# Block-distance products for the inner weights of gated linear attention, and paired weight halves in two small projections

## The chip, the cores and the metric

The kernel runs on one core of a Trainium2 chip. The metric is device microseconds from launch to end; three runs gave 1918.55, 1923.94 and 1927.39 us, median 1923.94 us.

## The reference

One layer of a hybrid decoder: 1024 prompt tokens and 64 sample tokens (8 sequences of 8), 1088 in all, model width 1024. After adaLN and an RMSNorm one input projection feeds two head groups: gated linear attention (GLA, 4 heads, keys of 64, values of 128) and a sparse attention of 8 heads with compressed blocks, selected blocks and a window. One output projection joins them; a squared-ReLU MLP follows. What the change touches:

```
logf = log_sigmoid(za @ gla_w_gate + gla_b_gate) / 16          # za: 16 columns of the input projection
chunks of 16 tokens:  b = cumsum(logf);  q_in = q*exp(b);  k_in = k*exp(-b);  k_out = k*exp(b_last - b)
a_intra = causal(q_in @ k_in^T)                                # within a chunk of 16
s = s*exp(b_last) + k_out^T v                                  # state carried from chunk to chunk
hid = silu(z_first + z_second + b1);  kc, vc = hid @ w2 + b2   # compressed keys and values
gates = sigmoid(zg)                                            # 24 gate columns of the input projection
```

## The kernel before

TensorE has no fast product of two f32 operands of full precision, so most products are split: `split` (L250) writes a high part in fp32r (ScalarE, L251) and the remainder in fp32r (VectorE, L252), and `mm3` (L254) issues three matmuls, high x high, low x high, high x low (L257, L258, L259; which operand is the weight varies). Plain f32 matmuls are used for small things; in the trace a plain f32 matmul is two records, a transpose one.

The eight PSUM banks go by tag (`bank`, L232): two `mm`, two `dn`, three `g`, one `av`. A tile asked for under a tag waits until an older one of that tag is free. The order of the instructions on every engine is set by a planner that simulates the program in time; the two GLA functions stand under a high priority, so that their instructions are taken as soon as they can run, and the projections fill what TensorE has left.

- `first_phase` (L342) compresses the samples' cached pages: for each of 8 sequences, one key half and one value half. The value half ends with `hid @ w2` (L519): for each of 2 heads and 2 halves f of the hidden width an `mm3` with the hidden tile as weight and 64 columns of `w2` moving, twelve matmuls of 64 columns, then one VectorE addition of the bias into `vc` and two DMAs on POOL's queue. Loads of the adaLN weight (`w_ada`, 512 KB each) run beside it. `cw2h` and `cw2l` hold the high and low part of `w2`; the value part is stored twice side by side. `compressed_keys` (L1017) has the same twelve matmuls once for the prompt.
- `project_gla` (L731) projects token chunks of 384, 384 and 320 columns. The unit `w_za` has 56 weight columns (16 for `za`, 16 unused, 24 gates): 24 matmuls per chunk by `mm3`. ScalarE copies 16 rows into `za` (whose 17th row is ones, for the bias) and takes the tanh of 24 rows; transposes (L743) turn the gates into token rows in a `dn` bank, which VectorE turns into `gates` (L753). The first chunk is projected while the other two are still being normed.
- `gla` (L828) works through the 1024 tokens in 8 tiles of 128. `log_decay` (L813) forms the decay for two tiles by f32 matmuls of 17 rows (L820). From cumulative sums it makes `eb`, `enb`, `eo` (`k_out`), the block sums `E`, and `QB`, the scaled queries with each head's rows alone. The 128x128 weights of a tile, for 4 heads, go block by block: for each pair p of heads, one VectorE product makes `KI`, 128 keys as each of the 8 query blocks sees them (128x1024, L883); POOL overwrites the 8 own blocks with `enb` (L886); 8 f32 matmuls have one [128x128] slice of `KI` as weight and 32 columns of `QB` moving (2 heads x 16 queries, L888). Four predicated copies (L893) put the causal part into `A`, which is zero elsewhere. Then follow output (L898, L900), norm, transposes (L915) and the state (L919, L924, L931).
- Around these tiles TensorE does the rest of `project_gla` and `project_kv`, in `mm` banks.

The lines of the inner weights:

```
for j in range(8):
    nc.gpsimd.tensor_copy(KI[:, j, j], enb[:, p, 16 * j:16 * j + 16])
for j in range(8):
    nc.tensor.matmul(pa[:, p, j], KI[:, j].rearrange("p a b -> p (a b)"), QB[:, p, j], start=True, stop=True)
```

Of the kernel before, what the change touches and what calls it, by code (L numbers as in the profile page):

```python
# [9 lines left out]
F32 = mybir.dt.float32  # L10
F32R = mybir.dt.float32r
# [30 lines left out]
def shape_constants():  # L42
# [22 lines left out]
    c["causal"] = (j <= i).astype(np.float32)  # L65
# [8 lines left out]
    c["ones"] = np.ones((128, 128), np.float32)  # L74
    return c, big
# [144 lines left out]
class Prog:  # L220
# [121 lines left out]
    def first_phase(self):  # L342
        nc, tc, a = self.nc, self.tc, self.a
        with ExitStack() as st:
# [42 lines left out]
            def tables():  # L387
# [5 lines left out]
                self.split(self.cw2h, self.cw2l, w2)  # L393
                pos = self.small[:, 162:194].rearrange("p (k t) -> p k t", k=2)
# [53 lines left out]
            def compress(b, kind, first):  # L448
# [64 lines left out]
                else:  # L513

                    ps = self.bank("g")
                    x = [y.rearrange("p f (h n) -> p f h n", h=2) for y in (hh, hl)]
                    for h in range(2):
                        for f in range(2):
                            self.mm3(ps[:, h * 64:(h + 1) * 64], [y[:, f, h] for y in x],  # L519
                                     (self.cw2h[:, 1, f, :64], self.cw2l[:, 1, f, :64]), f == 0, f == 1)  # L520
                    vc = t([128, 128], "vc", bufs=1)
                    nc.vector.tensor_tensor(vc, ps[:, :128], self.small[:, 34:162], op=OP.add)
# [3 lines left out]
            for i, (b, kind) in enumerate([(b, kind) for b in range(6) for kind in range(2)] + [(6, 0), (7, 0), (6, 1), (7, 1)]):  # L526
# [12 lines left out]
                if 2 <= i < 14:  # L539
                    ada_chunk(i - 2)  # L540

# [83 lines left out]
    def main_phase(self):  # L625
        nc, tc, a = self.nc, self.tc, self.a
        ffn = ExitStack()
        with ExitStack() as top:
# [3 lines left out]
            with ExitStack() as left, ExitStack() as mid:  # L632
# [5 lines left out]
                self.za = self.t(gp, [17, NT], F32, "za")  # L638
# [92 lines left out]
    def project_gla(self, pool, xs):  # L731
# [3 lines left out]
        for cis in (slice(0, 1), slice(1, 3)):  # L735
            F = lambda i: zip(self.feat_linear(a["w_f"][i], 128, xs[cis]), CHUNKS[cis])
            for ps, (c0, npr, n) in zip(self.feat_linear(a["w_za"], 56, xs[cis]), CHUNKS[cis]):
                nc.scalar.copy(self.za[:16, c0:c0 + n], ps[:16])
                gt = self.t(pool, [128, 384], F32, "st", 2)[:24, :n]
                nc.scalar.activation(gt, ps[32:56], AF.Tanh, scale=0.5)  # L740
                for o in range(0, n, 128):
                    w = min(128, n - o)
                    nc.tensor.transpose(pg[:w, (c0 + o) // 128], gt[:, o:o + w], self.C("ident")[:24, :24])  # L743
# [8 lines left out]
        for d, x in ((self.gates, pg[:, :8]), (self.gates_s, pg[:NS, 8])):  # L752
            nc.vector.tensor_scalar(d, x, 0.5, 0.5, op0=OP.mult, op1=OP.add)  # L753
# [74 lines left out]
    def gla(self, st):  # L828
# [3 lines left out]
        self.wg = t([17, 256], "wg")  # L832
        nc.sync.dma_start(self.wg, self.a["wg"])
        QBs, As, qis = ([t(sh, f"{x}{i}") for i in range(k)]
                        for sh, x, k in (([128, 2, 8, 2, 16], "QB", 2), ([128, 4, 128], "A", 2),
                                         ([128, 2, 2, 8, 16], "qi", 1)))
# [881 lines left out]
```

## Time and profile before

| | |
|---|---|
| median of three runs | 1923.94 us (1918.55 to 1927.39) |
| profiled execution | 1928.44 us, span 1926.8 us |
| TensorE matmul records | 1834.3 us busy, 12185 |
| VectorE / ScalarE / GpSimd busy | 1131.1 / 935.2 / 361.6 us |
| mean granted TensorE clock | 0.965 of full speed |
| DMA | 246 MB, mean 128 GB/s |

Times are microseconds from the start of the span. Engines: PE is the matmuls of TensorE, PEld its weight loads, DVE VectorE, ACT ScalarE, POOL GpSimd. Matmuls overlap: the duration printed for one holds its way through the array, so the time from one start to the next is what one costs in a row of them. PEclk is the granted clock as a share of full speed; a stretch at 0.50 runs at 1.2 GHz, one at 1.00 at 2.4 GHz.

### The profile page before, as it was taken

The numbers are of one execution on the slowest core, as the hardware profiler recorded it, in microseconds if no ns is written. First come the engines' busy times: TensorE is split into PE (matmuls) and PEld (weight loads), VectorE is DVE, ScalarE is ACT, GpSimd is POOL, SyncE is SP. The second block draws the span as 40 slices with busy tenths as digits, with TensorE's granted clock in tenths as the row PEclk, the third lists the DMA queues.
The fourth block names the chain that finished last, engine by engine and source line by source line (L and its number), as shares of the span: only waits on it lengthen the run. The fifth ranks groups of instructions, "written<-read, shape, count | busy, mean of one in ns | idle before, by whom it ended". The sixth has DMA issues, their size and how long they took to land.

```text
span 1926.8 us, 33628 instructions
## 1 busy us (share of the span) xinstructions
PE 1834.3 (95%) x12185; PEld 1645.7 (85%) x12185; DVE 1131.1 (59%) x2499; ACT 935.2 (49%) x1889; POOL 361.6 (19%) x622
## 2 busy tenths in 40 slices
PE   4999999999999999999999899999999999999997
PEld 4888889999989756456687699899999999999996
DVE  7866775355433574345545746956566668755555
ACT  4423354243333477366655656534433464654443
POOL 4433202124410355245222200000000001000000
PEclk8999999989999899699999899999999999999998
DMA  7667641103464504233112356412121245664442
GB/s 252 217 233 237 210 137 45 34 31 102 142 211 154 187 12 140 68 111 110 50 59 66 105 191 195 145 55 77 44 88 56 76 155 159 206 203 153 149 148 93
DMA packets 117149, 246.01 MB, mean 128 GB/s; under 512 B 14443, under 2 KB 72589, under 8 KB 116182
## 3 DMA queue, kind: packets, MB, share of 16 engines
q1 hardware_dynamic: 101206, 196.98, 32.4%
q0 software_dynamic: 13328, 43.99, 6.6%
q10 hardware_dynamic: 2448, 2.88, 0.4%
q8 instruction: 96, 1.57, 0.3%
q14 instruction: 71, 0.58, 0.1%
HBM read 215.88 MB, written 32.05 MB: 129 GB/s over the span
## 4 chain that ended last, share of the span: by engine, by line
PE 80%; DMA 6%; DVE 6%; ACT 3%; issue 3%; SPq 1%; POOL 1%; POOLq 0%; ACTq 0%; DVEq 0%
PE mm L257 11%; PE mm L259 11%; PE mm L258 11%; PE dn L257 5%; PE dn L258 5%; PE dn L259 5%; PE av L1154 4%; PE g L1149 4%; PE g L258 3%; PE g L257 3%; PE g L259 3%; PE dn L1126 2%; DMA wr<-w_ada 2%; PE dn L1127 2%; PE mm L1296 1%
## 5 line engine op out<-in xcount | busy, mean ns | idle before, releaser
L252 DVE TENSOR_TENSOR wl<-wr,wh 128x1024 fp32r<-128x1024 f32 (+1 forms) x176 | 215.0, 1222 | 202.0 <-ACT wh L251 200.6
L251 ACT CAST wh<-wr 128x1024 fp32r<-128x1024 f32 (+1 forms) x176 | 183.3, 1042 | 239.4 <-PE mm L258 111.2
L257 PE MATMUL dn<-fh,wh 128*128 128x384 f32 (+1 forms) x616 | 206.3, 336 | 2.6 <-DVE fo L1559 1.7
L258 PE MATMUL dn<-fl,wh 128*128 128x384 f32 (+1 forms) x616 | 205.5, 334 | 0.0
L259 PE MATMUL dn<-fh,wl 128*128 128x384 f32 (+1 forms) x616 | 205.2, 334 | 0.0
L586 POOL TENSOR_TENSOR rs_r<-rs_m,mhalf 128x2 f32<-128x2 f32 (+2 forms) x12 | 12.9, 1078 | 709.6 <-DVE rs_m L585 709.5
L257 PE MATMUL mm<-hT,wh 128*128 128x384 f32 (+3 forms) x408 | 138.2, 339 | 5.3 <-DVE st L765 3.3
L258 PE MATMUL mm<-hT,wh 128*128 128x384 f32 (+3 forms) x408 | 136.8, 335 | 0.0
L259 PE MATMUL mm<-hT,wl 128*128 128x384 f32 (+3 forms) x408 | 136.7, 336 | 0.0
L257 PEld LDWEIGHTS dn<-fh,wh 128*128 128x128 f32 x616 | 115.7, 188 | 4.7 <-DVE fo L1559 2.7
L258 PEld LDWEIGHTS dn<-fl,wh 128*128 128x128 f32 x616 | 115.7, 188 | 0.3 <-DVE fl L252 0.3
L259 PEld LDWEIGHTS dn<-fh,wl 128*128 128x128 f32 x616 | 115.7, 188 | 0.1
L1151 ACT COPY pw<-g 128x512 f32<-128x512 f32 (+3 forms) x148 | 81.7, 585 | 59.9 <-PE g L1149 58.7
L1559 DVE TENSOR_TENSOR fo<-fo,dn 128x384 f32<-128x384 f32 (+1 forms) x134 | 72.4, 541 | 59.6 <-PE dn L259 58.9
L257 PE MATMUL mm<-w1h,wh 128*128 128x256 f32 x256 | 77.4, 302 | 19.8 <-ACT wh L251 14.9
L1154 PE MATMUL av<-pw,VV 128*64 128x256 f32 x528 | 86.8, 413 | 1.9 <-ACT pw L1151 1.8
L257 PEld LDWEIGHTS mm<-hT,wh 128*128 128x128 f32 (+1 forms) x408 | 77.0, 189 | 8.3 <-DVE st L765 4.4
L1126 PE MATMUL dn<-KK,QS 128*128 128x512 f32 (+3 forms) x192 | 77.7, 409 | 6.5 <-DVE mx L1129 6.3
L257 PE MATMUL mm<-cth,wh 128*128 128x256 f32 (+1 forms) x256 | 76.0, 298 | 5.2 <-ACT cth L251 4.7
L257 PE MATMUL mm<-x2h,wh 128*128 128x320 f32 x256 | 79.2, 309 | 0.0
L259 PE MATMUL mm<-x2h,wl 128*128 128x320 f32 x256 | 79.2, 309 | 0.0
L258 PE MATMUL mm<-x2l,wh 128*128 128x320 f32 x256 | 79.1, 309 | 0.0
(597 smaller groups left out, 5461.0 us busy)
## 6 DMA issues: line engine op xcount, KB each, us to landing
wr<-w_up SPq DMA_DIRECT2D x72, 512.0 KB, 3.6
wr<-w_down SPq DMA_DIRECT2D x72, 512.0 KB, 3.6
wr<-w_ada SPq DMA_DIRECT2D x48, 512.0 KB, 4.4
wr<-w_f SPq DMA_DIRECT2D x24, 512.0 KB, 3.8
wr<-cw SPq DMA_DIRECT2D x16, 512.0 KB, 4.4
wr<-w_out SPq DMA_DIRECT2D x16, 512.0 KB, 3.6
raw<-cc SPq DMA_DIRECT2D x62, 128.0 KB, 3.8
raw<-cc POOLq DMA_DIRECT2D x61, 128.0 KB, 4.9
```

The source lines that it names most:

```text
L251: return (self.nc.scalar.copy(h, src), (lo or self.nc.vector).tensor_tensor(l, src, h.bitcast(F32), op=OP.subtract))
L252: (lo or self.nc.vector).tensor_tensor(l, src, h.bitcast(F32), op=OP.subtract))
L257: mm(out, ah, bh, start=start, stop=False)
L258: mm(out, ah, bl, start=False, stop=False)
L259: mm(out, al, bh, start=False, stop=stop)
L1126: nc.tensor.matmul(ps, q, K[:, 0, c:c + cw], start=True, stop=False)
L1127: nc.tensor.matmul(ps, q, K[:, 1, c:c + cw], start=False, stop=True)
L1149: nc.tensor.transpose(pt[:, 128 * g:128 * g + 128], S[g][:, c:c + cw], self.C("ident"))
L1151: nc.scalar.copy(pw, pt)
L1154: nc.tensor.matmul(av[64 * j:64 * j + 64], V, pw.rearrange("p (a j q) -> p j a q", a=2, j=2)[:, j], start=first and c == 0, stop=last and ...
L1296: mm(ps[64 * b2:64 * b2 + 64], self.Q[:, 2 * pr + b2], keys(b2), start=False, stop=True)
L1559: nc.vector.tensor_tensor(o, o, ps, op=OP.add)
```

## The change

Inner weights by distance. Query block and key block of a tile are grouped by how far up the binary tree of the 8 blocks they part. Own block: `enb` x `QB`. Neighbour in the same pair: `eo` x the odd blocks of `QB`. Other pair of the same four: `k2` x `q2`. Other half of the tile: `k4` x `q4`. `k2`, `k4`, `q2`, `q4` carry the decay to a boundary between the two blocks. For each pair of heads that is four f32 matmuls with a [128x128] weight and 256, 128, 128 and 128 moving columns, in place of eight with 32. `KI` and POOL's copies go; nine small VectorE products per tile come; the four predicated copies become one over 512 columns and one over 256, and ScalarE makes three plain copies. The results take three `g` banks (`p0`, `p12`, `p3`) instead of one.

Paired halves. The unit `w_za` becomes one tile of 120 columns: high part, 8 zeros, low part. A chunk takes 16 matmuls instead of 24: the low part of x against the high columns, the high part of x against all 120. All 120 rows go into `za`; `wg` gets 128 rows with the gate weight twice, so that `log_decay` adds both halves. The gates leave `za` by an f32 matmul with a 0/1 table `pick` (128 rows, 24 columns) in place of a transpose; one tanh over all gates at the end replaces one per chunk. `cw2h` gets high and low part side by side: `hid @ w2` takes 8 matmuls instead of 12 (four of 128 columns, four of 64), and two VectorE additions instead of one.

```diff
-                    nc.vector.tensor_tensor(vc, ps[:, :128], self.small[:, 34:162], op=OP.add)
+                    nc.vector.tensor_tensor(v, ps[:, :, 0], self.small[:, 34:162].rearrange("p (h d) -> p h d", h=2), op=OP.add)
+                    nc.vector.tensor_tensor(v, v, ps[:, :, 1], op=OP.add)
...
+    def values2(self, ps, x):
+        w = self.cw2h[:, 1]
+        for f in range(2):
+            if f == 1:
+                self.nc.tensor.matmul(ps[:, 0], x[1][1], w[:, 1, :64], start=False, stop=False)
+            self.nc.tensor.matmul(ps.rearrange("p i d -> p (i d)"), x[0][f], w[:, f], start=f == 0, stop=f == 1)
+            if f == 0:
+                self.nc.tensor.matmul(ps[:, 0], x[1][0], w[:, 0, :64], start=False, stop=False)
...
-            for ps, (c0, npr, n) in zip(self.feat_linear(a["w_za"], 56, xs[cis]), CHUNKS[cis]):
-                nc.scalar.copy(self.za[:16, c0:c0 + n], ps[:16])
-                nc.scalar.activation(gt, ps[32:56], AF.Tanh, scale=0.5)
-                    nc.tensor.transpose(pg[:w, (c0 + o) // 128], gt[:, o:o + w], self.C("ident")[:24, :24])
+            nc.vector.memset(w[:, :, 56:64].bitcast(F32), 0.0)
+            self.split(w[:, :, :56], w[:, :, 64:120], r)
+            for x, (c0, npr, n) in zip(xs[cis], CHUNKS[cis]):
+                ps = self.bank("mm")[:120, :n]
+                for k in range(8):
+                    if k == 7:
+                        nc.tensor.matmul(ps[:56], w[:, k, :56], x[1][:, k], start=False, stop=False)
+                    nc.tensor.matmul(ps, w[:, k, :120], x[0][:, k], start=k == 0, stop=k == 7)
+                    if k < 7:
+                        nc.tensor.matmul(ps[:56], w[:, k, :56], x[1][:, k], start=False, stop=False)
+                nc.scalar.copy(self.za[:120, c0:c0 + n], ps)
+                    nc.tensor.matmul(pg[:m, o // 128], self.za[:, o:o + m], self.C("pick"), start=True, stop=True)
...
+            for m in (0, 4):
+                nc.vector.tensor_tensor(k2[:, :, m:m + 2], e4[:, :, m:m + 2],
+                                        E[:, :, m + 2, m:m + 2, None].to_broadcast([128, 2, 2, 16]), op=OP.mult)
+                for h in range(2):
+                    s = slice(64 * h, 64 * h + 64)
+                    nc.vector.tensor_tensor(q2[s, :, h, m // 4], QB[s, :, h, m + 2:m + 4],
+                                            E[s, :, m + 2:m + 4, m + 1:m + 2].to_broadcast([64, 2, 2, 16]), op=OP.mult)
+            nc.vector.tensor_tensor(k4[:, :, :4], e4[:, :, :4], E[:, :, 4, :4, None].to_broadcast([128, 2, 4, 16]), op=OP.mult)
+            for h in range(2):
+                s = slice(64 * h, 64 * h + 64)
+                nc.vector.tensor_tensor(q4[s, :, h], QB[s, :, h, 4:], E[s, :, 4:8, 3:4].to_broadcast([64, 2, 4, 16]),
+                                        op=OP.mult)
             for p in range(2):
-                KI = t([128, 8, 8, 16], "KI", 2)
-                nc.vector.tensor_tensor(KI, e4[:, p, None].to_broadcast([128, 8, 8, 16]),
-                                        E[:, p, :8, :, None].to_broadcast([128, 8, 8, 16]), op=OP.mult)
-                for j in range(8):
-                    nc.gpsimd.tensor_copy(KI[:, j, j], enb[:, p, 16 * j:16 * j + 16])
-                for j in range(8):
-                    nc.tensor.matmul(pa[:, p, j], KI[:, j].rearrange("p a b -> p (a b)"), QB[:, p, j],
-                                     start=True, stop=True)
+                nc.tensor.matmul(p0[:, p], enb[:, p], QB[:, p].rearrange("p h j t -> p (h j t)"), start=True, stop=True)
+                q1 = QB[:, p].rearrange("p h (m o) t -> p o (h m) t", o=2)[:, 1]
+                nc.tensor.matmul(p12[:, 0, p].rearrange("p (x t) -> p x t", t=16), eo[:, p], q1, start=True, stop=True)
+                nc.tensor.matmul(p12[:, 1, p], k2[:, p].rearrange("p j t -> p (j t)"),
+                                 q2[:, p].rearrange("p h m j t -> p (h m j t)"), start=True, stop=True)
+                nc.tensor.matmul(p3[:, p], k4[:, p].rearrange("p j t -> p (j t)"),
+                                 q4[:, p].rearrange("p h j t -> p (h j t)"), start=True, stop=True)
-            for h in range(4):
-                nc.vector.copy_predicated(A[:, h].rearrange("p (i t) -> p i t", t=16),
-                                          causal.rearrange("p (i t) -> p i t", t=16), pa[:, h // 2, :, h % 2])
+            nc.vector.copy_predicated(A, own, p0.rearrange("p a (h n) -> p (a h) n", h=2))
+            nc.vector.copy_predicated(A.rearrange("p h (m o t) -> p o h m t", o=2, t=16)[:, 1], odd,
+                                      p12[:, 0].rearrange("p a (h m t) -> p (a h) m t", h=2, t=16))
+            for m in range(2):
+                s = slice(64 * m, 64 * m + 32)
+                nc.scalar.copy(A[s, :, 64 * m + 32:64 * m + 64],
+                               p12[s, 1].rearrange("p a (h m n) -> p m (a h) n", h=2, m=2)[:, m])
+            nc.scalar.copy(A[:64, :, 64:], p3[:64].rearrange("p a (h n) -> p (a h) n", h=2))
```

## Rows read from the trace of the kernel before

**Rows 1.** The page's busy time of each engine over the span.
```profile
PE 1834.3 (95%) x12185; PEld 1645.7 (85%) x12185; DVE 1131.1 (59%) x2499; ACT 935.2 (49%) x1889; POOL 361.6 (19%) x622
```

**Rows 2.** The chain that ended last, shares of the span by engine.
```profile
PE 80%; DMA 6%; DVE 6%; ACT 3%; issue 3%; SPq 1%; POOL 1%; POOLq 0%; ACTq 0%; DVEq 0%
```

**Rows 3.** Busy time by stage: engine busy (instructions), then PEclk, DMA share, GB/s.
```profile
285.00:520.00 235.00, 234.05 (x1656) 226.18 (x1654) 116.03 (x259) 90.68 (x222) 62.30 (x175) 0.96 0.20 64
...
660.00:820.00 160.00, 152.31 (x907) 91.66 (x908) 82.40 (x380) 98.30 (x298) 73.71 (x133) 0.83 0.26 82
```

**Rows 4.** What PE waited for, 285 to 520 us: total, times, longest.
```profile
PE mm L257 <- ACT vt L756: 0.3, 1, 0.3
```

**Rows 5.** PE's timeline in one GLA tile: start, length, line, shapes, count.
```profile
399.79 0.39 PE L898 MATMUL dn<-vt,A 128*128 128x128 f32 x2
...
400.68 1.03 PE L924 MATMUL av<-vt,kt 128*128 128x256 f32 x4
401.55 0.63 PE L849 MATMUL g<-cst,lf 128*128 128x138 f32 x4
...
410.86 3.65 PE L888 MATMUL g<-QB,KI 128*128 128x32 f32 x32
414.35 0.41 PE L919 MATMUL av<-cst,ko 128*128 128x128 f32 x2
```

**Rows 6.** Busy time and granted clock behind five of GLA's eight tiles.
```profile
317.00:322.00 5.00, 5.00 (x19) 4.42 (x19) 2.38 (x7) 3.31 (x5) 0.00 (x0) 0.66 0.03 8
...
386.00:394.00 8.00, 8.00 (x35) 6.90 (x35) 2.43 (x8) 2.23 (x10) 0.00 (x0) 0.57 0.00 0
411.00:419.00 8.00, 8.00 (x69) 8.00 (x68) 5.49 (x13) 3.70 (x9) 2.64 (x12) 1.00 0.19 68
...
430.00:435.00 5.00, 5.00 (x24) 4.77 (x23) 1.54 (x3) 4.11 (x7) 0.28 (x1) 0.66 0.00 0
...
464.00:469.00 5.00, 5.00 (x27) 4.90 (x27) 0.90 (x4) 1.06 (x2) 0.00 (x0) 0.66 0.40 138
```

**Rows 7.** Lines of GLA's inner weights, 285 to 520 us: busy, mean ns.
```profile
L886 POOL COPY KI<-enb 128x16 f32<-128x16 f32 x128 | 30.2, 288 | 75.4 <-DVE KI L883 70.2 <-PE mm L259 5.2
...
L883 DVE TENSOR_TENSOR KI<-eo,E 128x1024 f32<-128x1024 f32 x16 | 18.9, 1220 | 0.3
...
L893 DVE COPY_PREDICATED A<-cst,g 128x128 f32<-128x128 int32 x32 | 7.3, 297 | 26.0 <-PE g L888 17.9 <-PE dn L898 8.2
```

**Rows 8.** PE's timeline where the unit w_za is projected, third chunk.
```profile
287.21 0.30 PE L258 MATMUL mm<-hT,wh 128*56 128x320 f32 x1
...
290.40 0.31 PE L259 MATMUL mm<-hT,wl 128*56 128x320 f32 x1
290.64 0.36 PE L743 MATMUL dn<-cst,st 24*128 24x24 f32 x3
290.93 0.44 PE L257 MATMUL mm<-hT,wh 128*128 128x384 f32 x1
```

**Rows 9.** PE's timeline in the decay's matmuls of 17 rows.
```profile
429.16 1.13 PE L820 MATMUL g<-wg,za 17*128 17x256 f32 x4
430.22 0.49 PE L258 MATMUL mm<-hT,wh 128*128 128x384 f32 x1
```

**Rows 10.** PE's timeline: a sample's value product, then the prompt's key product.
```profile
71.62 0.27 PE L257 MATMUL g<-cw2h,hh 128*128 128x64 f32 x1
...
72.51 0.28 PE L259 MATMUL g<-cw2h,hl 128*128 128x64 f32 x1
...
581.06 0.28 PE L259 MATMUL g<-chh,cw2l 128*128 128x126 f32 x1
...
581.40 0.27 PE L259 MATMUL g<-chh,cw2l 128*128 128x126 f32 x1
```

**Rows 11.** What PE waited for, 60 to 285 us.
```profile
PE dn L428 <- DMA wr<-w_ada: 8.3, 6, 2.2
PE av L594 <- DVE sq L601: 3.5, 1, 3.5
```

More of the change, by code (lines that the diff above doesn't have):

```diff
@@ L64, in shape_constants @@
     c["tri"] = np.concatenate([tri, bi], 1)
[L65 removed]
+    m, q = np.arange(64)[None, :] // 16, p[:, None] // 16
+    c["odd"] = (q == 2 * m).astype(np.float32)
     m8 = np.zeros((128, 64), np.float32)
@@ L393, in tables @@
                 self.split(self.cw2h, self.cw2l, w2)
+                nc.scalar.copy(self.cw2h[:, 1, :, 64:], self.cw2l[:, 1, :, :64].bitcast(F32))
                 pos = self.small[:, 162:194].rearrange("p (k t) -> p k t", k=2)
@@ L831, in gla @@
         t = lambda shape, tag, bufs=1, dt=F32: self.t(pool, shape, dt, tag, bufs)
[L832 to L836, printed above, removed]
-        for x in QBs + As + qis:
+        self.wg = t([128, 256], "wg")
+        nc.vector.memset(self.wg, 0.0)
+        for o in (0, 64):
+            nc.sync.dma_start(self.wg[o:o + 16], self.a["wg"][:16])
+        nc.sync.dma_start(self.wg[120:121], self.a["wg"][16:])
+        QBs, As, qis, q2s, q4s, k2s, k4s = ([t(sh, f"{x}{i}") for i in range(k)]
+                        for sh, x, k in (([128, 2, 2, 8, 16], "QB", 2), ([128, 4, 128], "A", 2),
+                                         ([128, 2, 2, 8, 16], "qi", 1), ([128, 2, 2, 2, 2, 16], "q2", 2),
+                                         ([128, 2, 2, 4, 16], "q4", 2), ([128, 2, 8, 16], "k2", 2), ([128, 2, 8, 16], "k4", 2)))
+        for x in QBs + As + qis + q2s + q4s + k2s + k4s:
             nc.gpsimd.memset(x, 0.0)
-        causal = self.C("causal").bitcast(I32)
+        own = self.C("tri")[:, :128].bitcast(I32)[:, None].to_broadcast([128, 4, 128])
+        odd = self.C("odd").bitcast(I32).rearrange("p (m t) -> p m t", t=16)[:, None].to_broadcast([128, 4, 4, 16])
         for i in range(8):
@@ L842, in gla @@
                 lfs = self.log_decay(pool, TILES[i:i + 2])
-            QB, A, qi = QBs[i % 2], As[i % 2], qis[0]
+            QB, A, q2, q4, k2, k4, qi = (x[i % 2] for x in (QBs, As, q2s, q4s, k2s, k4s, qis * 2))
             first = i == 0
@@ new lines, in gla @@
+            nc.vector.tensor_tensor(k4[:, :, :4], e4[:, :, :4], E[:, :, 4, :4, None].to_broadcast([128, 2, 4, 16]), op=OP.mult)
[3 more added lines that the diff above has]
+                                        op=OP.mult)
+            p0 = self.bank("g").rearrange("p (a n) -> p a n", a=2)
+            p12 = self.bank("g").rearrange("p (l a n) -> p l a n", l=2, a=2)
@@ L1068, in compressed_keys @@
             else:
-                pv = self.bank("g")[:nb, :128]
+                pv = self.bank("g")[:nb, :256].rearrange("p (h i d) -> p h i d", h=2, i=2)
                 for h in range(2):
-                    for f in range(2):
-                        x = [y[:, f].rearrange("p (c h) -> p h c", h=2)[:, h] for y in (hh, hl)]
-                        self.mm3(pv[:, 64 * h:64 * h + 64], x, (self.cw2h[:, 1, f, :64], self.cw2l[:, 1, f, :64]),
-                                 f == 0, f == 1)
-                nc.vector.tensor_tensor(self.VC[:nb].rearrange("p h d -> p (h d)"), pv, self.small[:nb, 34:162], op=OP.add)
+                    self.values2(pv[:, h], [[y[:, f].rearrange("p (c h) -> p h c", h=2)[:, h] for f in range(2)]
+                                            for y in (hh, hl)])
+                v = self.VC[:nb]
+                nc.vector.tensor_tensor(v, pv[:, :, 0], self.small[:nb, 34:162].rearrange("p (h d) -> p h d", h=2), op=OP.add)
+                nc.vector.tensor_tensor(v, v, pv[:, :, 1], op=OP.add)
             yield
```

27 lines of the change are left out of this document (15 added, 12 removed).

## The prediction

> **What bounds the kernel now.** I read the busy times first, then the chain that ended last, then the stages, then what TensorE (PE) waits for. PE's matmuls are busy 95% of the span [rows 1], and the chain of waits runs through PE for 80% of it [rows 2]. In the stage that holds the GLA tiles, 285 to 520 us, PE is busy 234.05 of 235 us, and its longest wait is 0.3 us [rows 3, 4]. VectorE, ScalarE and POOL have half of that stage or more to spare [rows 3]. So a PE microsecond taken out there comes off the end, and work that moves on VectorE, ScalarE and POOL costs nothing as long as it delays no PE instruction. Before 265 us this holds only in part: PE waits there for the w_ada loads (8.3 us) and once 3.5 us for VectorE, just before the second norm [rows 11]; what PE saves ahead of such a wait lengthens the wait.
>
> **The change, part by part.** Where PE works without a break, a matmul costs the time from its start to the next start.
>
> *A. Inner weights, PE.* The old block runs from 410.86 to 414.35: 3.49 us, 32 records of 0.109 us (16 f32 matmuls, two records each) [rows 5]. New are two f32 matmuls with 256 moving columns and six with 128 per tile. The 256-column price is L924: four records, two matmuls, from 400.68 to 401.55, so 0.435 us a matmul. The 128-column price is the run of four pairs (L898, L900 by turns) from 399.79 to 400.68, 0.2225 us a matmul [rows 5]. The sum is 2 x 0.435 + 6 x 0.2225 = 2.2 us, and 3.49 - 2.2 = 1.29 us saved, in 8 tiles 10.3 us. Bounds: if all 16 new records went at the 0.109 us of the old ones, a block would be 1.74 us and the saving 14 us; if the operands in pieces of 16 queries made each matmul as long as a printed pair, 0.39 us, the block would be 3.1 us and the saving 3 us. I keep 10.3, since L898 to L924 have the same sizes, type and neighbours.
>
> *B. The clock behind the old block.* Behind four of the eight old blocks the granted clock falls to 1.2 GHz for some microseconds; behind the others, as from 411 to 419 us, it stays at 2.4 GHz [rows 6]. PE was not idle before the falls: it was in the 32-column block or had just left it. Lost is length times (1 - clock): 5 x 0.34, 8 x 0.43, 5 x 0.34 and 5 x 0.34, together 8.5 us. L898 to L924, the shapes that take the block's place, also run as a block of 8 x 0.2225 + 0.87 = 2.65 us in each tile, and in 411 to 419, which holds one, no fall is seen. If the new block behaves like them, most falls go. But the longest fall, 386 to 394, is filled with exactly these shapes at the low clock, so I count two thirds of the loss: 5.7 us, bounds 0 and 8.5.
> Here the Trainium skill (TensorE: Matmul & The Clock Gate, table "Why this matters for your kernels") says otherwise: it puts drops in the middle of a kernel down to gaps in which PE is idle between bursts of matmuls. By that rule B would be 0, since the block has no gap, and the sum below 12.6 us in place of 18.3. The trace speaks against it: the drops come with PE busy 5.00 of 5.00 us and 8.00 of 8.00 [rows 6]; but it does not show that the new block is free of them.
>
> *C. The w_za unit.* A 320-column matmul costs (290.40 - 287.21)/22 = 0.145 us [rows 8]; by columns, one of 384 costs 0.174. Gone are 8 per chunk: 8 x (2 x 0.174 + 0.145) = 3.9 us. The first chunk's 1.4 us lie ahead of the 3.5 us wait [rows 11], so half of it counts: 3.2 us. The nine picks cost more than the nine transposes: a transpose takes (290.93 - 290.64)/3 = 0.097 us [rows 8], a narrow f32 matmul with a 128-column weight 2 x 0.109 = 0.218 us [rows 5], so 9 x 0.121 = 1.1 us. Net 2.1 us, bounds 1.4 and 2.8. The wider copy into `za`, the memset, the one late tanh and the second small load of `wg` are ScalarE, VectorE and DMA work beside a PE that is full; if ScalarE were late, the next weight unit's high part would be late, and PE's longest wait in this stage is 0.3 us, for another copy [rows 4].
>
> *D. Compressed values.* Eight samples lose 4 matmuls each. A 64-column one costs (72.51 - 71.62)/8 = 0.111 us; the 126-column ones of the prompt's keys cost (581.40 - 581.06)/3 = 0.113 us, so the wider ones that remain are no dearer [rows 10]. 32 x 0.111 = 3.6 us, before 265 us, where waits take back a part; I count half, 1.8 us, bounds 0 and 3.6. The prompt's four lie in the noise. The extra VectorE addition delays only `vc` and its DMAs on POOL's queue, read back only in the samples' attention.
>
> *E. The decay's matmuls* go from 17 rows to 128. With 17 rows two matmuls of 256 columns take 430.22 - 429.16 = 1.06 us [rows 9], against 0.87 us for L924 with 128 rows [rows 5]. Four pairs and one more: 4.5 x 0.19 = 0.8 us saved, by the row nearest to the new shape; bounds 0 and 0.8. The Trainium skill (TensorE: Matmul & The Clock Gate, Part 2) says that the number of rows does not enter into the time of a weight load; by that E would be 0 and the sum 17.5. The two prices differ [rows 5, 9], but stand at different places of the program, so they do not decide it.
>
> *F. The other engines and the three banks.* VectorE loses two products of 1.22 us and four copies of 0.297 us per tile [rows 7], 3.6 us; it gains nine products over 768 columns in all (0.9 us at the old product's time per column, at most 9 x 0.3 = 2.7 us) and two copies over 768 columns (1.8 us at the old copy's): 2.7 to 4.5 us, about even. POOL loses 3.8 us per tile. ScalarE gains three copies, some 0.4 us each by the same copy, 1.2 us against 144 us that it has free in the stage [rows 3]. What can cost is that `p0`, `p12` and `p3` fill all three `g` banks: the next tile's cumulative sums, which now start right behind the block (L849 at 401.55 stands behind L924, and a second `g` bank is free) must wait until `A` is filled, at least 1.2 us of VectorE later. PE runs its queue in order; if the planner has put such a matmul too early, everything behind it stands. I allow one wait of the size of PE's longest in this stage [rows 4] per tile, 8 x 0.3 = 2.4 us of loss; bounds 0 and, if each tile stood for both new copies, 8 x 1.8 = 14 us.
>
> Sum: 10.3 + 5.7 + 2.1 + 1.8 + 0.8 - 2.4 = 18.3 us. The profiled execution took 1928.44 us (span 1926.8) and goes to 1910.1; it lies 4.5 us above the median of the runs, 1923.94, and the median is what I forecast: 1905.6, so 1906 us.
>
> **Rivals.**
> *R1, the clock stays as it is and the early savings drown.* B is 0, because the falls are not the old block's doing or because the new block, plain f32 like it, brings them too; with D at 0 as well the sum is 10.3 + 2.1 + 0.8 - 2.4 = 10.8 us: 1913 us. For it: the long fall filled with 128-column f32 work; the waits before 265 us [rows 11]. Against it: no fall in 411 to 419 [rows 6]. Chance 0.20. The rule of the Trainium skill (TensorE: Matmul & The Clock Gate) on idle gaps would lead to this case.
> *R2, another order costs time elsewhere.* The planner's times change from the first value product on, so the order of everything behind is drawn anew. The attention stage, 660 to 820 us, has a mean clock of 0.83 [rows 3]: 160 x 0.17 = 27 us are lost there, a sum that hangs on how PE's work lies. If the loss grows by half, 13.5 us, the time is 1919; if it shrinks by half, 1892. For it: PE falls there without any line of the change near. Against: the same work with the same needs. Chance 0.13 for the worse, 0.06 for the better.
> *R3, slower: the three banks.* If PE stands behind a matmul that waits for a `g` bank, the price is per tile: the copies into `A`, then the chain of cumulative sum, exponentials and products of the next tile, which the trace shows from 401.55 to the block's start at 410.86, 9.3 us [rows 5], normally under projections. From 2.6 us of standing per tile (20.7/8, the sum without F) nothing is gained; from 3.8 us the kernel is slower by over half a per cent; at 5 us it takes 1923.9 - 20.7 + 40 = 1943 us. For it: before, only one of three banks was held at this point. Against it: the projections have their own `mm` banks, and the planner knows the banks. Chance 0.07.
> The change not doing what it says would be the new block at 3 us or more, the lower bound of A: it is inside R1's range, not a case of its own.
>
> **How the numbers follow.** The forecast has 0.54, its own range 1896 to 1913 (A to E at their upper bounds without F would be 1894; B at 0 gives 1911). With 0.20, 0.13, 0.06 and 0.07 this makes 1. Half a per cent, 9.6 us, is about what a measurement of this kernel tells from no change: 1914.3 and 1933.6. Faster: nearly all of the forecast (0.53), just over half of R1 (0.11) and the better draw (0.06), 0.70. Same: the rest of R1, the worse draw and a little of R3, 0.22. Slower: most of R3 and the tail of the worse draw, 0.08. The range 1890 to 1921 leaves out R3, a part of the worse draw and the best draws.
>
> **What would show it.** A: the block's time in the GLA stage, 2.2 us per tile in place of 3.49. B: stretches below clock 1.00 between 285 and 500 us, one or two in place of four. C and D: 48 matmuls in the w_za unit, eight per value product, each at the old price. F: PE's waits for VectorE or ScalarE copies of `A`, under 3 us in all. The GLA stage as a whole should shrink by about 17 us. I am wrong if that stage is not at least 10 us shorter, or if it is and the end does not follow because the attention stage gives it back.

## The result and the profile after

The changed kernel takes 1903.83 us (median of four runs, 1900.82 to 1905.83) against 1925.66 us for the kernel before on the same chip (four runs, 1918.55 to 1935.06): a ratio of 0.9865, 95% interval 0.9822 to 0.9908. The forecast was 1906 us. Repeated on another chip it took 1903.41 us, ratio 0.9872 (0.9824 to 0.992). Ratios leave out slow runs, those more than 1.5% above the fastest of their kernel, so they differ a little from the ratio of the medians printed. The profiled execution took 1902.94 us, its span is 1901.3 us, 25.5 us shorter than the 1926.8 us of before; the mean granted clock rose from 0.965 to 0.970.

The page's busy times and the chain by engine, after, against [rows 1, 2]:

```profile
PE 1798.7 (95%) x12006; PEld 1617.3 (85%) x12006; DVE 1130.0 (59%) x2551; ACT 938.8 (49%) x1913; POOL 333.9 (18%) x502
...
PE 77%; issue 7%; DVE 7%; DMA 5%; ACT 2%; POOL 1%; SPq 1%; POOLq 0%; DVEq 0%; ACTq 0%
```

PE lost 35.6 us of busy time, VectorE 1.1, POOL 27.7, ScalarE gained 3.6; the chain still runs through PE for 77%. To see where the span became shorter I read the start of the last matmul of three lines: the spread of the second norm (the front ends), the samples' state products (the GLA stage ends), the attention's scores. First before, then after (line, count, min/median/max ns, first to last start, shapes):

```profile
L594 PE MATMUL av<-cst,r x18: 271/275/550, 227.7 to 266.7; 128*128 128x128 f32 x16, 64*128 64x64 f32 x2
L1009 PE MATMUL g<-vl,km x16: 278/279/416, 501.8 to 519.6; 128*128 128x256 f32 x16
L1126 PE MATMUL dn<-KK,QS x192: 221/408/735, 655.5 to 1067.9; 128*128 128x512 f32 x88, 128*128 128x128 f32 x56, 128*128 128x384 f32 x24, 128*128 128x256 f32 x24
```

```profile
L607 PE MATMUL av<-cst,r x18: 272/275/550, 228.9 to 267.9; 128*128 128x128 f32 x16, 64*128 64x64 f32 x2
L1060 PE MATMUL g<-vl,km x16: 278/280/415, 477.2 to 497.6; 128*128 128x256 f32 x16
L1177 PE MATMUL dn<-KK,QS x192: 219/408/775, 634.5 to 1042.5; 128*128 128x512 f32 x88, 128*128 128x128 f32 x56, 128*128 128x384 f32 x24, 128*128 128x256 f32 x24
```

The front ends 1.2 us later. The GLA stage takes 497.6 - 267.9 = 229.7 us in place of 252.9, 23.2 less. What lies behind it takes 1901.3 - 497.6 = 1403.7 us in place of 1407.2, 3.5 less. So nine tenths of the 25.5 us are in the stage that was changed. (A small part of it is only the border: counted over the timelines, 8 fewer projection matmuls of 256 columns, 0.116 us each, stand in the stage after, 0.9 us.) The same reading of every profiled kernel (us; "with" names the parts of the change in it):

| kernel | with | front ends | GLA stage | behind it |
|---|---|---|---|---|
| before | none | 266.7 | 252.9 | 1407.2 |
| after | all | 267.9 | 229.7 | 1403.7 |
| after, repeated | all | 268.1 | 230.9 | 1404.6 |
| e1 | inner weights | 272.8 | 237.5 | 1401.1 |
| e2 | w_za unit, decay | 266.0 | 245.7 | 1405.8 |
| e3 | values | 267.2 | 248.9 | 1404.8 |
| e4 | all but values | 265.8 | 230.0 | 1407.0 |
| e5 | all, + narrow block | 270.3 | 258.5 | 1401.8 |
| e6 | all, + wide block | 268.6 | 253.9 | 1430.2 |
| e7 | all, + VectorE work | 270.0 | 236.5 | 1392.5 |
| e8 | all, POOL in the front | 263.8 | 230.1 | 1410.8 |
| e9 | e8 without values | 269.2 | 231.1 | 1431.0 |
| e11 | all, wide sample block | 266.0 | 228.9 | 1404.0 |
| e12 | e11 without values | 261.5 | 233.0 | 1400.6 |

Stages of the profile after, as in [rows 3], and a stretch with a whole block in it:

```profile
285.00:500.00 215.00, 214.38 (x1531) 209.35 (x1531) 114.72 (x300) 95.19 (x246) 32.79 (x48) 0.98 0.22 71
640.00:800.00 160.00, 153.13 (x989) 95.10 (x989) 84.78 (x404) 105.07 (x320) 77.07 (x141) 0.91 0.28 88
...
301.00:309.00 8.00, 8.00 (x57) 7.89 (x56) 5.02 (x16) 3.20 (x10) 0.00 (x0) 1.00 0.21 68
```

What PE waited for in 285 to 500 us, and then the longest waits in 60 to 285 us, after:

```profile
PE mm L259 <- ACT vt L781: 0.3, 1, 0.3
PE mm L260 <- DVE wl L254: 0.2, 1, 0.2
```

```profile
PE dn L431 <- DMA wr<-w_ada: 10.0, 5, 2.6
PE av L607 <- DVE sq L614: 4.8, 1, 4.8
```

In the stage no wait is for the copies of `A` or for a `g` bank [rows 4]. In the front the two waits of [rows 11] are there again and longer, 14.8 us in place of 11.8.

PE's timeline with the new block of one tile, after, in the place of [rows 5]:

```profile
301.60 0.59 PE L929 MATMUL g<-QB,enb 128*128 128x256 f32 x2
302.03 0.38 PE L931 MATMUL g<-QB,eo 128*128 128x128 f32 x2
302.25 0.60 PE L929 MATMUL g<-QB,enb 128*128 128x256 f32 x2
302.50 0.52 PE L259 MATMUL mm<-hT,wh 128*128 128x384 f32 x1
302.86 0.34 PE L260 MATMUL mm<-hT,wh 128*128 128x384 f32 x1
...
304.38 0.38 PE L932 MATMUL g<-q,k 128*128 128x128 f32 x2
...
305.27 0.39 PE L934 MATMUL g<-q,k 128*128 128x128 f32 x2
305.50 0.38 PE L970 MATMUL av<-cst,ko 128*128 128x128 f32 x2
```

The first three matmuls take 0.90 us, and the projection matmul that overlaps the third stands 0.18 us longer than its like (302.50 to 302.86 against 0.175). The five others (five pairs from 304.38 to 305.50) take 1.12 us. That is 2.2 us, 0.43 for 256 columns and 0.22 for 128. Projections were put between the two groups: the matmuls with `k2` to `q4` need nine VectorE products more than the first ones.

The w_za unit, third chunk, with the decay and the picks behind it, against [rows 8, 9]:

```profile
286.76 0.31 PE L763 MATMUL mm<-hT,wh 128*56 128x320 f32 x1
...
287.34 0.31 PE L761 MATMUL mm<-hT,wh 128*120 128x320 f32 x1
287.49 1.02 PE L845 MATMUL g<-wg,za 128*128 128x256 f32 x4
288.35 0.74 PE L767 MATMUL dn<-cst,za 128*128 128x24 f32 x6
288.94 0.42 PE L259 MATMUL mm<-hT,wh 128*128 128x384 f32 x1
```

A w_za matmul costs 0.145 us (four in 0.58) with 120 weight columns as with 56, a decay pair 0.86 us, a pick 0.59/3 = 0.20 us.

### The profile page after: what moved, and what is told of

Same layout as the page of the kernel before. It is cut to its first block, busy times and chain, and to the rows that moved or that the text cites. A ratio compares the mean times of both kernels' runs of the same rounds, so it can differ in the third digit from the quotient of the medians.

```text
span 1901.3 us, 33235 instructions
## 1 busy us (share of the span) xinstructions
PE 1798.7 (95%) x12006; PEld 1617.3 (85%) x12006; DVE 1130.0 (59%) x2551; ACT 938.8 (49%) x1913; POOL 333.9 (18%) x502
## 4 chain that ended last, share of the span: by engine, by line
PE 77%; issue 7%; DVE 7%; DMA 5%; ACT 2%; POOL 1%; SPq 1%; POOLq 0%; DVEq 0%; ACTq 0%
PE mm L259 10%; PE mm L260 10%; PE mm L261 10%; PE dn L259 5%; PE dn L260 5%; PE dn L261 5%; PE g L1200 4%; PE av L1205 4%; PE g L260 3%; PE g L259 3%; PE g L261 3%; PE dn L1177 2%; DMA wr<-w_ada 2%; PE dn L1178 2%; PE mm L1347 1%
## 5 line engine op out<-in xcount | busy, mean ns | idle before, releaser
L254 DVE TENSOR_TENSOR wl<-wr,wh 128x1024 fp32r<-128x1024 f32 x174 | 213.2, 1225 | 215.4 <-ACT wh L253 214.0
L259 PE MATMUL mm<-hT,wh 128*128 128x384 f32 (+1 forms) x384 | 128.7, 335 | 6.0 <-ACT st L801 3.4
L260 PE MATMUL mm<-hT,wh 128*128 128x384 f32 (+1 forms) x384 | 128.1, 334 | 0.0
L261 PE MATMUL mm<-hT,wl 128*128 128x384 f32 (+1 forms) x384 | 127.4, 333 | 0.4 <-DVE wl L254 0.4
L259 PEld LDWEIGHTS mm<-hT,wh 128*128 128x128 f32 x384 | 73.4, 191 | 7.9 <-ACT st L801 3.6
```

The source lines that it names most:

```text
L254: (lo or self.nc.vector).tensor_tensor(l, src, h.bitcast(F32), op=OP.subtract))
L259: mm(out, ah, bh, start=start, stop=False)
L260: mm(out, ah, bl, start=False, stop=False)
L261: mm(out, al, bh, start=False, stop=stop)
```

## The experiments

Each was timed beside the kernel before on the same chip. A "fall" is a stretch with PE busy in which the granted clock goes from 2.4 to 1.2 GHz. The stages are read from one profiled execution of each kernel.

**e1, the inner weights alone.** The kernel before with the new tables, products, eight matmuls and copies of `gla`, and nothing else of the change:

```diff
-                for j in range(8):
-                    nc.tensor.matmul(pa[:, p, j], KI[:, j].rearrange("p a b -> p (a b)"), QB[:, p, j],
...
+                nc.tensor.matmul(p0[:, p], enb[:, p], QB[:, p].rearrange("p h j t -> p (h j t)"), start=True, stop=True)
...
```

> The kernel before with the inner weights by block distance alone. Theory (the block itself is worth 8 x 1.29 = 10.3 us, and the four clock falls behind the old block, 8.5 us, go with it): 18 to 19 us faster than before, ratio near 0.990; no stretch under 1.2 GHz in the GLA stage behind the new block, one may stay behind the samples' 16-column matmuls. Rival (the falls lie where the order of the work puts them, not behind the narrow block): 10 us faster, ratio near 0.9945, and falls still in the GLA stage.

Measured: 1915.87 us, ratio 0.9941 (0.9911 to 0.997); the kernel before had 1928.74 on this chip. The gain, by the ratio 11.4 us, is the rival's. The trace says otherwise: behind the eight blocks the clock stays at 1.00, and the stage is 15.4 us shorter. But the front of this profile ends 6.1 us later than that of before, with no line of the edit in it, so the rival's reason, falls that remain, is not what kept the time up. (What lies behind the stage is 6.1 us shorter, so this profile as a whole gained the stage's 15.4 us; the ratio's interval is 5.7 us either way.) The one fall left in the stage comes behind the samples' matmuls of 16 columns (windows as in [rows 3]):

```profile
484.00:492.00 8.00, 8.00 (x43) 8.00 (x43) 2.24 (x3) 3.31 (x3) 0.00 (x0) 0.59 0.37 133
```

**e2, w_za and decay alone; e3, the values alone.** The kernel before, each with its own part of the change:

```diff
# e2
-            for ps, (c0, npr, n) in zip(self.feat_linear(a["w_za"], 56, xs[cis]), CHUNKS[cis]):
+            for x, (c0, npr, n) in zip(xs[cis], CHUNKS[cis]):      # 16 matmuls; za of 128 rows, pick, wg of 128 rows
# e3
-                        self.mm3(ps[:, h * 64:(h + 1) * 64], ...)
+                        self.values2(ps[:, h], [[y[:, f, h] for f in range(2)] for y in x])
```

> The kernel before with the paired w_za unit, the picks, the late tanh and the 128-row gate weight alone. Theory: 2 to 3.5 us faster (24 matmuls less, nine picks, 4.5 decay pairs at 0.87 instead of 1.06 us), ratio 0.998 to 0.999; the old block of 3.49 us is there and clock falls stand behind several of its eight places. Rival (the order drawn anew moves the time by more than the edit): over 5 us either way.

> The kernel before with the eight-matmul value products alone. Theory (VectorE sets the pace from 225 to 267 us, so PE time saved there is lost in the wait ahead of the second norm, and the second addition is eight times 0.29 us more on VectorE): 0 to 1.5 us slower, ratio 1.000 to 1.001; the last spread of a norm before the GLA stage starts no earlier than 266 us. Rival (PE is the bound of the first stage too): 3.6 us faster, that spread about 263 us.

Measured: e2 1920.93 us, ratio 0.9981 (0.9954 to 1.0009); e3 1923.91 us, 0.9968 (0.9941 to 0.9995). e2 agrees. e3 is faster than the theory said, but not where its rival put it: its front ends at 267.2 us, not before the 266.7 of before, though the value products are cheaper. Of the 5.9 us that its profile gained, 4.0 lie in the GLA stage, in which no line of it works. Four old blocks of e2 were followed by a fall, one of e3 (windows of 8 us; the first and the last of e2, those between being 380 to 388 and 408 to 416 at the same 0.79; then that of e3):

```profile
320.00:328.00 8.00, 8.00 (x44) 7.78 (x44) 2.44 (x7) 3.98 (x7) 0.00 (x0) 0.79 0.23 66
...
452.00:460.00 8.00, 8.00 (x54) 7.96 (x54) 2.20 (x8) 1.74 (x5) 2.17 (x3) 0.79 0.15 52
```

```profile
408.00:416.00 8.00, 7.62 (x44) 7.51 (x44) 5.16 (x14) 2.01 (x7) 2.09 (x9) 0.79 0.39 131
```

Each costs 8 x 0.21 = 1.7 us. In the window of e3, and in e2's from 408 to 416 us, PE is busy 7.62 of 8.00 us: one wait of 0.38 us stands inside the block, just before the fall. So the same block is sometimes followed by a fall and sometimes not.

**e4, all but the values.** The changed kernel with `mm3` in place of `values2`:

```diff
-                        self.values2(ps[:, h], [[y[:, f, h] for f in range(2)] for y in x])
+                            self.mm3(ps[:, h * 64:(h + 1) * 64], [y[:, f, h] for y in x], ...)
```

> The changed kernel with the twelve-matmul value products of before. Theory (as for the value products alone): as fast as the changed kernel or up to 1.5 us faster, ratio to before 0.986 to 0.988. Rival (the value products give their 3.6 us): 3 us slower than the changed kernel, ratio near 0.990.

Measured: 1899.64 us, ratio 0.9852 (0.9816 to 0.9887), as fast as the whole change. The waits in the front are shorter by about what the products take longer: 7.2 us for `w_ada` and 4.3 for VectorE, against 10.0 and 4.8 after:

```profile
PE dn L430 <- DMA wr<-w_ada: 7.2, 5, 2.8
PE av L596 <- DVE sq L603: 4.3, 1, 4.3
```

The parts don't add up in the whole time: by the ratios e1 and e2 gain 11.4 and 3.7 us, e4, which holds both, 28.5. The intervals are 5 to 7 us either way each; the rest of that difference is not settled. In the GLA stage they do add up: e1 takes 15.4 us off it and e2 7.2, together 22.6, and e4 takes off 22.9.

**e5 and e6, the same PE time added in narrow and in wide matmuls.** The changed kernel, with extra products behind the block in each tile, into an unused part of the third bank; they are not read:

```diff
# e5
+            for x in range(16):
+                nc.tensor.matmul(b3[:, 256:288], enb[:, x % 2], QB[:, x % 2, 0, :2]..., start=True, stop=True)   # 32 columns
# e6
+            for x in range(8):
+                nc.tensor.matmul(b3[:, 256:512], enb[:, x % 2], QB[:, x % 2]..., start=True, stop=True)   # 256 columns
```

> The changed kernel with 16 more f32 matmuls in each GLA tile, 32 moving columns each, into an unread half of the third bank: the shape of the old block, 3.49 us a tile, 28 us in all. Theory (a run of such narrow matmuls is what the clock falls follow): falls to 1.2 GHz in the GLA stage again, behind two to five of the eight tiles, and 31 to 37 us more than the changed kernel, 1935 to 1941 us. Rival (falls come from the length of plain f32 work or from where the order puts the work, whatever the width): the same falls as with the wide extra matmuls, and the same time.

> The changed kernel with 8 more f32 matmuls in each GLA tile, 256 moving columns each: 8 x 0.435 = 3.48 us a tile, the same PE time as the narrow ones, 28 us in all. Theory: no clock fall behind a tile, 28 us more than the changed kernel, 1932 us. Rival (length of plain f32 work): falls behind several tiles, as with the narrow ones, and their time.

Measured: e5 1937.02 us, ratio 1.0017 (0.9982 to 1.0052); e6 1945.99 us, 1.0077 (1.0052 to 1.0103); the extra blocks take 28.1 and 27.6 us of PE. In e5 two of eight blocks were followed by a fall. One of the two, PE's timeline and then the stretch:

```profile
340.82 3.66 PE L938 MATMUL g<-QB,enb 128*128 128x32 f32 x32
344.32 0.36 PE L259 MATMUL mm<-wh,hT 128*128 128x256 f32 x1
344.52 0.28 PE L260 MATMUL mm<-wl,hT 128*128 128x256 f32 x1
...
344.76 0.42 PE L259 MATMUL mm<-wh,hT 128*128 128x256 f32 x1
...
348.17 0.28 PE L260 MATMUL mm<-wl,hT 128*128 128x256 f32 x1
```

```profile
344.00:348.00 4.00, 4.00 (x24) 4.00 (x24) 0.00 (x0) 0.37 (x1) 0.00 (x0) 0.59 0.01 2
```

The narrow block has just ended, no gap stands in the rows, and a projection matmul goes from a length of 0.28 us to 0.42, and is back at 0.28 from 348.17 on. In e6 no block is followed by a fall, and the clock of its stage rounds to 1.00; its attention's stays low:

```profile
285.00:500.00 215.00, 214.51 (x1462) 206.19 (x1460) 97.87 (x269) 88.25 (x234) 22.31 (x31) 1.00 0.17 56
640.00:800.00 160.00, 151.62 (x892) 103.70 (x893) 88.25 (x360) 98.04 (x292) 67.44 (x125) 0.85 0.33 103
```

So the falls go with the theory. In the stage itself e5 takes 4.6 us more than e6 (258.5 against 253.9): 3.4 us of that are e5's two falls, and about 1.6 us are 14 projection matmuls more. The whole times do not decide: by the ratios e5 takes some 29 us more than the changed kernel, where the theory had 31 to 37, and e6 some 41, where it had 28. In its profile e6 is slower because the stages behind GLA take 26.5 us longer than after (1430.2 against 1403.7). They hold 33 projection matmuls more, which in the profile of after stand in the GLA stage (3.8 us); of the rest 13.2 us go to a lower clock and 10.3 us to longer waits of PE. The order behind the extra products is another, but the profiled execution (1954.37 us) is also the slowest of e6's eight, so how much of this is the order's doing is not settled.

**e7, VectorE's old work put back.** The changed kernel, with about 2.8 us of products per tile that are not read:

```diff
+            for c in range(4):
+                KI = t([128, 4, 8, 16], "KI", 1)
+                nc.vector.tensor_tensor(KI, e4[...].to_broadcast([128, 4, 8, 16]), E[...].to_broadcast([128, 4, 8, 16]), op=OP.mult)
```

> The changed kernel with four more VectorE products of 512 columns in each GLA tile, unread, between the inner products and the copies into A: 4 x 0.7 = 2.8 us a tile, 22 us of VectorE in all, more than the old product cost. Theory (VectorE, ScalarE and POOL lie beside a full PE in that stage): the time of the changed kernel within 3 us, PE's waits in the stage under 3 us. Rival (the three filled banks make the next tile wait for VectorE, and PE with it): 10 us or more slower, PE waiting in the GLA stage for the copies or for the next tile's work.

Measured: 1901.21 us, ratio 0.9861 (0.9825 to 0.9897), the time of the changed kernel. PE waits 1.9 us in 285 to 500 us, none of it at the tiles' banks: the two waits of after, and 1.4 us at the samples' state products, behind the tiles:

```profile
PE g L1064 <- DVE km L1060: 1.4, 1, 1.4
...
```

So 2.8 us more of VectorE per tile cost no time that can be told. The stage is 6.8 us longer in this profile than in that of after: 26 projection matmuls more stand in it (3.0 us), its clock is low at the end (0.68 from 484 to 500 us; 1.9 us more are lost to the clock than after), and there is the wait of 1.4 us. What follows is 11.2 us shorter.

**e8 and e9, is it VectorE that holds the front?** In the first chunk POOL makes the low parts of the weights in place of VectorE; e9 is the same with the old value products:

```diff
-            F = lambda i: zip(self.feat_linear(a["w_f"][i], 128, xs[cis]), CHUNKS[cis])
+            lo = nc.gpsimd if cis.start == 0 else None
+            F = lambda i: zip(self.feat_linear(a["w_f"][i], 128, xs[cis], lo), CHUNKS[cis])
-            self.split(w[:, :, :56], w[:, :, 64:120], r)
+            self.split(w[:, :, :56], w[:, :, 64:120], r, lo)
```

> The changed kernel with the low parts of the five weight units of the first token chunk (w_za and four w_f units) made on POOL instead of VectorE. Theory (VectorE sets the pace from 225 to 267 us): about 5 us of VectorE work less there, the last norm spread of the stage starts 3 to 5 us earlier than 266.5 us and the whole is 2 to 5 us faster than the changed kernel, 1899 to 1902 us. Rival (the loads or PE set the pace, or POOL's slower product delays the weights): no gain, the spread within 1 us of where it was.

> The changed kernel with the value products of before and the low parts of the first token chunk's five weight units on POOL. Theory (VectorE paces the first stage, and less VectorE work there comes off the end): the last norm spread before 263 us, 3 to 5 us faster than the changed kernel beside it. Rival (the order behind the GLA stage is drawn anew with every edit and is worth as much as that): the spread as early, the whole within 3 us of the changed kernel or slower.

Measured: e8 1908.79 us, ratio 0.9896 (0.9861 to 0.9932); e9 1916.64 us, 0.9982 (0.9945 to 1.002). In e8 the front ends 4.1 us earlier, as expected; in e9 it ends at 269.2, 3.4 us later than in e4, from which e9 differs by this edit alone, against the theory. So whether VectorE sets the end of the front stays open. Neither became faster than the changed kernel, as the theories had it. Both profiles lose behind the GLA stage, 7.1 and 27.3 us against after, at a lower clock in the attention (e8, then e9; e9's profiled execution took 1932.93 us, 16 us more than the median of its runs):

```profile
640.00:800.00 160.00, 152.89 (x884) 93.37 (x884) 78.99 (x366) 94.48 (x288) 68.14 (x125) 0.80 0.26 80
```

```profile
640.00:800.00 160.00, 152.96 (x830) 94.40 (x829) 77.47 (x356) 92.95 (x291) 68.87 (x131) 0.74 0.28 88
```

**e10, the changed kernel again**, beside e9, e11 and e12 on one chip, without an edit:

> The changed kernel once more, beside the other three of this set. Both theories: 1901 to 1906 us, ratio to before 0.985 to 0.989.

Measured: 1903.41 us (six runs, 1900.83 to 1908.32), as given above.

**e11, the samples' 16 columns made wide.** After, one fall is left in the stage, behind the samples' old-style block. First its rows, then the clock behind it:

```profile
472.36 4.67 PE L1030 MATMUL dn<-QB,s 128*128 128x16 f32 x32
476.87 0.56 PE L1060 MATMUL g<-vh,km 128*128 128x256 f32 x1
```

```profile
474.00:476.00 2.00, 2.00 (x15) 2.00 (x15) 0.00 (x0) 0.11 (x1) 0.00 (x0) 0.74 0.98 385
476.00:478.00 2.00, 2.00 (x10) 2.00 (x11) 1.02 (x2) 1.98 (x2) 0.00 (x0) 0.50 0.18 74
...
480.00:482.00 2.00, 2.00 (x10) 2.00 (x10) 1.86 (x3) 1.66 (x3) 0.00 (x0) 0.55 0.03 8
```

e11 gives each of these matmuls 128 columns: masked copies of the queries, summed over the samples.

```diff
+        nc.gpsimd.memset(QM, 0.0)
+        for j in range(8):
+            nc.gpsimd.tensor_copy(QM[:, j, :, 8 * j:8 * j + 8], QB...[:, :, 8 * j:8 * j + 8])
-                                  QB[:, p, :, 8 * j:8 * j + 8], start=True, stop=True)
+                                  QM[:, j, 2 * p:2 * p + 2]..., start=j == 0, stop=j == 7)
```

> The changed kernel with the samples' 32 records of 16 moving columns widened to 128: the queries of each sequence alone in a tile of zeros, accumulated over the eight sequences. The PE time is the same, since a record of 128 columns starts 0.111 us after the last one and one of 16 columns 0.109. Theory (the clock falls behind runs of narrow matmuls; it fell behind this one in all ten profiles so far): no fall behind the samples' products, about 3.4 us faster than the changed kernel beside it. Rival (the fall belongs to the place, where the projections run out, not to the width): the fall stays.

Measured: 1901.74 us, ratio 0.9862 (0.9814 to 0.9909). Block and next matmuls, then the clock up to 479 us and beyond:

```profile
470.50 3.84 PE L1034 MATMUL dn<-QM,s 128*128 128x128 f32 x32
474.09 0.36 PE L1064 MATMUL g<-vh,km 128*128 128x256 f32 x1
...
478.92 0.63 PE L592 MATMUL dn<-cst,g_sq 128*64 128x2 f32 x8 [0.89 <-ACT g_sq L1040]
```

```profile
470.00:479.00 9.00, 8.12 (x69) 7.84 (x67) 3.92 (x4) 5.35 (x7) 0.00 (x0) 1.00 0.38 140
480.00:484.00 4.00, 4.00 (x19) 3.77 (x20) 3.77 (x7) 0.12 (x1) 1.99 (x3) 0.58 0.35 90
```

128 columns cost no more than 16 did (3.59 us start to start against 4.51 with the fall in it), and the fall behind the block is gone; another comes from 480 us on, after PE had waited 0.89 us and had run eight matmuls of 2 columns. It costs 1.7 us, as much as the one behind the samples' block in the repeated changed kernel on the same chip (from 478.0 to 481.4 us), so the rival, that the fall belongs to the place, is not excluded for these matmuls. The GLA stage, 228.9 us, is 0.8 us shorter than after, less than can be told, and so is the whole: 1.7 us under the changed kernel beside it, with runs that overlap, where the theory had 3.4.

**e12, e11 without the value part.** e11 with e4's edit, both diffs as above:

> Both at once: value products of before, samples' products widened. Theory: no fall behind the samples' products; 3 to 5 us faster than the changed kernel beside it, 1896 to 1900 us. Rival: the fall stays, and the time lies within 2 us of the changed kernel.

Measured: 1898.24 us (six runs, 1894.67 to 1906.6), ratio 0.9855 (0.9804 to 0.9906). It is the lowest of the four medians on this chip, 5.2 us under the changed kernel's, but the runs of the two overlap, so I do not call it faster. Its fall, at 482 to 489 us, follows a wait of 1.33 us.

## Why the prediction was right, step by step

Direction, size and place were right: 1906 forecast, 1903.83 measured, and the stage became 23.2 us shorter where some 17 were forecast, with one low stretch between 285 and 500 us in place of four (the one left is the samples'; before, theirs lies at 502 us).

*A, right.* 2.2 us per block, as priced; 10.3 us. e1, which has A and B alone, takes 15.4 us off the stage.

*B, right in its cause, mis-sized for this pair of profiles.* Blocks of 32 columns were followed by a fall 11 times in 32 (before 4, e2 4, e3 1, e5 2, of 8 each); blocks of 128 and 256 columns alone in none of 80 (after, e1, e4, e6 to e12). From the profile of before all four went, 8.5 us, the upper bound. Part of it came back: the fall behind the samples' block costs 3.4 us after, 1.7 before (and 1.7 in the repetition of after, so this varies with the execution). The falls are not there each time: before lost 8.5 us to them, e2 6.7, e3 1.7, on average 5.6, which is what I had put down for another reason: that the size came out is luck. What I held against the step, the long fall full of 128-column work, was the tail of a fall and not its cause: it begins at 386.1 us, while the block of 32 columns that started at 383.0 still ran. How much of the spread of whole runs is theirs the runs don't tell: e2, with four falls in its profile, ranged over 9 us, e1, with none behind a tile, over 17. The Trainium skill (TensorE: Matmul & The Clock Gate, table "Why this matters for your kernels") puts drops down to gaps between bursts, and these falls are not of that kind: e5's begins in rows without a gap. Other falls at the stage's end come behind waits of PE: 0.89 us in e11, 1.33 in e12, 1.4 in e7 and 2.6 in e4; what made them stays open, since no run took those waits away.

*C, right in price.* 48 matmuls at 0.145 us and by columns, picks at 0.20 us where I had 0.218. In the stage that is 16 matmuls, 2.5 us, less 0.9 us for the nine picks. The half of the first chunk that I counted, 0.7 us, lies in the front, which did not become shorter. e2 has C and E alone: 7.2 us off the stage, of which 2.2 were forecast there and 3.6 are 31 projection matmuls of 256 columns that its order puts beyond the stage's border.

*E, right for a pair, but misread and too small.* A decay pair takes 0.86 us after, where I had 0.87. In all three profiles with 17 rows that I read at this place (before, e1, e3) the first pair takes 1.06 us, in all three with 128 rows (after, e2, e4) 0.86. But a weight load of 17 rows is not slower: it lasts 0.18 us, one of 128 rows 0.19. The Trainium skill (TensorE: Matmul & The Clock Gate, Part 2) says that the number of rows does not enter into the time of a weight load, and the trace agrees. Inside a pair, too, the records start 0.216 us apart with either (the first one of 17 rows takes 0.32). The difference stands at the two ends of the group. PEld, the weight loads, waits ahead of the loads of 17 rows and again behind them, and not around those of 128 rows (before, then after):

```profile
429.16 0.72 PEld L820 LDWEIGHTS g<-wg,za 17*128 17x128 f32 x4 [0.17 <-issue]
430.21 0.19 PEld L258 LDWEIGHTS mm<-hT,wh 128*128 128x128 f32 x1 [0.33 <-issue]
```

```profile
287.34 0.77 PEld L845 LDWEIGHTS g<-wg,za 128*128 128x128 f32 x4
288.14 0.85 PEld L767 LDWEIGHTS dn<-cst,za 128*128 128x128 f32 x6
```

So a load of 17 rows, and the load of 128 rows behind it, were not begun under the matmul before them; why, no run shows. The rule of the Trainium skill is about the length of the load alone, so E need not be 0 by it, as I had put it. The price comes once for a group of decay matmuls. Five groups of e3 that run at the full clock carry 0.24 to 0.30 us of it each, so my estimate of E is 1.4 us in place of 0.8.

*D, the wrong term: 0 in place of 1.8.* The two waits of the front grew by 3.0 us, nearly the 3.6 saved, and e4 is as fast without the part. I had counted half; it was R1's second half that held.

*F, 0 in place of 2.4.* PE never waits for a `g` bank in the stage, and the planner puts projections between the two groups of the new block. e7 shows how much room VectorE has. R3 did not come.

So the stage's terms come to 10.3 (A) + 8.5 - 1.7 (B, less the samples' fall) + 1.6 (C) + 1.4 (E) + 0.9 (border) = 21.0 us against 23.2. Another 0.5 us is an earlier low stretch, which reaches 3.3 us into the stage before and 2.3 after; 1.7 us stay unexplained. The forecast of 18.3 was a little short because the profile of before lost more to the clock than I counted, E was larger and F was nothing; D and the front's part of C went the other way. That F's 2.4 and D's 1.8 nearly cancel is luck.

R2 did not decide this pair (3.5 us behind the stage), but its size is real: over the profiles above, what lies behind the stage takes from 1392.5 to 1431.0 us, with the same work in it but for up to 33 projection matmuls at the border either way (3.8 us). It made the profiles of e6 and e9 slow and hid e7's longer stage. Its cause, another order, is not shown. Most of the spread is the clock: its loss behind the stage (length times 1 - clock) is 29.8 us in e7, 40.7 after and 62.6 in e9. And one order alone can spread as far: the twelve runs of e9 range over 28 us, and their mean granted clock goes from 0.973 in the fastest to 0.957 in the slowest. R1's first half, falls that stay, did not come.

## What to carry to other kernels

When TensorE is full, give its matmuls the columns they can carry: eight products of 128 and 256 columns took 2.2 us where sixteen of 32 took 3.49, and the clock no longer fell behind them. Work taken out ahead of a wait for something else is not gained: look at the wait, not at the work. Where a planner orders the program, read the gain by stage before the total: in these profiles what lies behind the changed stage moved by up to 27 us with next to no edit in it.

## What the runs showed of the hardware that was not expected

A run of plain f32 matmuls of 32 columns is followed by a fall of TensorE's clock to 1.2 GHz in some executions (11 blocks in 32). The fall begins while the block runs or within 1.7 us of its end and costs 1.7 or 3.4 us. In nine of the eleven PE has no wait in the 6 us ahead of it; in the other two, of e2 and e3, there is one of 0.38 us inside the block. Behind 16 columns (the samples' block) a fall came in all 12 profiles that have that block. Widened to 128 columns the same number of matmuls took no longer (3.59 us in e11, 3.60 before at 2.4 GHz), and the fall behind them went, but another began some 6 us later. Two decay products of 256 columns took 1.06 us with 17 rows and 0.86 with 128, though a weight load lasts as long with either (0.18 and 0.19 us): the loads of 17 rows, and the load of 128 rows behind them, were not begun under the matmul before.
